# Attention weights transposed by VectorE blocks and GpSimd-queue transfers in place of TensorE, and the head norm's power moved to ScalarE and VectorE, in a hybrid decoder layer

## The chip, the cores and the metric

One core of a Trainium2 chip runs the whole program once. The metric is device microseconds of that core: the median of three runs of the kernel before is 1500.87 us (1500.5 to 1500.92). Everything is float32; the large matrix products are done as three float32r products of a high and a low part.

## The reference, cut to what matters

The program computes one decoder layer on 256 tokens of width 2048. The part that the diff touches is the two attentions of the mixer.

```python
# differential attention, 8 heads, per block of 128 queries
sc = einsum('bhmqd,bhmkd->bhmqk', qi, kh) * scale          # two maps m of width 64
p = softmax(where(causal, sc, -inf))
a = p[:, :, 0] - lam * p[:, :, 1]
o = einsum('bhqk,bhkv->bhqv', a, vh)                       # then rms_norm(o, da_subln_g)
# stick-breaking attention, 8 heads
z = einsum('bhqd,bhkd->bhqk', qi, kh) * scale
a = where(strict, exp(log_sigmoid(z) + tail), 0.0)
o = einsum('bhqk,bhkd->bhqd', a, vh)
```

Around them stand a projection of 2048 to 10240 columns, two branch projections with sigmoid gates, an output projection, a cross-attention, and a gated feed-forward part of width 5632 with a convolution over tokens.

## The kernel before, in words

The work is a stream of units. One unit multiplies the 256 tokens with 512 weight columns: 16 slices of 128 rows, two token tiles, three products each, so 96 matmuls of 512 columns. Weights come by SP's DMA queue in pieces of 1 MB; `split_w` makes the high part on ScalarE (L179) and the low part on VectorE (L180), in three buffers each; `multiply` issues the products (L185 to L187).

The attentions run as Python generators beside that stream. `product` calls `tick()` after every 12 matmuls, and a tick resumes at most two generators that are due; the number that a generator yields is the ticks until it is due again. That sets the order of the text. On every engine but SP the order of the program is then chosen when it is built, by Tile's scheduler, which goes by the text's order and by when it reckons each instruction to be ready (L723); on the chip each engine's order is fixed.

The units come in the order qa0, ka0, va0, qa1, ka1, va1, qb0, kb0, vb0, qb1, kb1, vb1, then eight gate units. Behind each qa and ka unit `proj_T` brings out the product, `rope` turns it with eight GpSimd instructions (L244 to L249), and two ticks later TensorE transposes it (L275). Behind va0 and va1 two chains of two heads each start, one tick apart; behind vb0 and vb1 one chain of two pairs of heads.

A head (`diff_head`) forms its scores (L312, four products, eight instructions on TensorE), masks them, takes the row maxima, the exponentials (L324) and the weights in place (L330, L332). Two ticks later `attn_T` transposes the three 128x128 blocks of weights on TensorE into PSUM (L294 to L296) and VectorE copies them out (L298). One tick on, the products with v follow (L341 to L343), the sum of squares (L160), the mean (L348), GpSimd's power of -1/2 (L351) and the scaling (L354); two ticks on, the result is transposed (L359). A pair of stick-breaking heads (`stick_pair`) does the same with other weights (L380 to L400), two calls of `attn_T`, and the products at L410 to L412.

In the feed-forward part the kernel already transposes another way: `turn` (L129) turns 32x32 blocks on VectorE, and `regroup` (L138) moves the blocks to their partitions with 16 DMAs from the GpSimd queue.

Tiles come from pools: `wk` has 7 buffers under the tag w2, `b4` has 34 of 4 KB a partition, `ps_sm` has 4 PSUM banks for scores, transposes and attention outputs.

Of the kernel before, what the change touches and what calls it, by code (L numbers as in the profile page):

```python
# [9 lines left out]
F32 = mybir.dt.float32  # L10
F32R = mybir.dt.float32r
AF = mybir.ActivationFunctionType
ALU = mybir.AluOpType
# [3 lines left out]
P = 128  # L17
S = 256
NT = S // P
# [26 lines left out]
def hybrid_layer(ctx: ExitStack, tc: tile.TileContext, x, xT, mem, memT, gmix, par, gfin,  # L46
                 w_in, w_pa, w_pb, w_out, w_xq, w_xkv, w_xo, w_up, w_dn, out):
    nc = tc.nc
# [58 lines left out]
    def chunk_tile(name, shape):  # L107
        return b4.tile(shape, F32, tag="b4", name=name)

    def sm_tile(name):  # L110
        return ps_sm.tile([P, U], F32, tag="sm", name=name)
# [175 lines left out]
            nc.scalar.activation(out=dst[:, t, :], in_=ps[t], func=AF.Copy, scale=r[:, t:t + 1])  # L287
        return dst

    def attn_T(a, name):  # L290


        pt = sm_tile(f"{name}_tp")
        nc.tensor.transpose(out=pt[:, 0:P], in_=a[0][:, 0:P], identity=ident)  # L294
        nc.tensor.transpose(out=pt[:, P:2 * P], in_=a[1][:, 0:P], identity=ident)
        nc.tensor.transpose(out=pt[:, 2 * P:3 * P], in_=a[1][:, P:2 * P], identity=ident)  # L296
        aT = wk.tile([P, 3 * P], F32, tag="w2", name=f"{name}_aT")
        nc.vector.tensor_copy(out=aT, in_=pt[:, 0:3 * P])  # L298
        return aT


    oaT = [None] * 4
# [1 line left out]
    def diff_head(h):  # L304
        qT, kT, v, hh = qa[h // 4], ka[h // 4], va[h // 4], h % 4

        at = (slice(0, P), slice(P, 3 * P))
        sc = [sm_tile(f"sa{m}") for m in range(2)]
        nm = st.tile([P, 2, NT], F32, tag="nm", name="nm")
        for m in range(2):  # L310
            for i in range(NT):
                nc.tensor.matmul(sc[m][:, at[i]], lhsT=qT[m * 64:(m + 1) * 64, hh, i * P:(i + 1) * P],  # L312
                                 rhs=kT[m * 64:(m + 1) * 64, hh, 0:(i + 1) * P], start=True, stop=True)
            dg = sc[m].rearrange("p (i k) -> p i k", i=2)[:, :, 0:P]
            nc.vector.tensor_tensor(out=dg, in0=dg, in1=mask_le.unsqueeze(1).broadcast_to([P, 2, P]),
                                    op=ALU.add)
            for i in range(NT):
                nc.vector.tensor_reduce(out=nm[:, m, i:i + 1], in_=sc[m][:, at[i]], op=ALU.max,
                                        axis=AX, negate=True)
        p = [wk.tile([P, 3 * P], F32, tag="w2", name=f"pa{m}") for m in range(2)]  # L320
        sm = st.tile([P, 2, NT], F32, tag="sm", name="sm")
        for m in range(2):
            for i in range(NT):
                nc.scalar.activation(out=p[m][:, at[i]], in_=sc[m][:, at[i]], func=AF.Exp,  # L324
                                     bias=nm[:, m, i:i + 1], scale=1.0, accum_out=sm[:, m, i:i + 1])
        nc.vector.reciprocal(out=sm, in_=sm)
        nc.vector.tensor_scalar(out=sm[:, 1], in0=sm[:, 1], scalar1=nlam, scalar2=None, op0=ALU.mult)
        aw = []
        for i in range(NT):
            nc.vector.tensor_scalar(out=p[0][:, at[i]], in0=p[0][:, at[i]], scalar1=sm[:, 0, i:i + 1],  # L330
                                    scalar2=None, op0=ALU.mult)
            nc.vector.scalar_tensor_tensor(out=p[0][:, at[i]], in0=p[1][:, at[i]],  # L332
                                           scalar=sm[:, 1, i:i + 1], in1=p[0][:, at[i]],
                                           op0=ALU.mult, op1=ALU.add)
            aw.append(p[0][:, at[i]])
        yield 2
        aT = attn_T(aw, "da")
        yield 1
        vc = slice(hh * P, (hh + 1) * P)
        po = sm_tile("oa").rearrange("p (t d) -> p t d", d=P)  # L340
        nc.tensor.matmul(po[:, 0], lhsT=aT[:, 0:P], rhs=v[:, 0, vc], start=True, stop=True)  # L341
        nc.tensor.matmul(po[:, 1], lhsT=aT[:, P:2 * P], rhs=v[:, 0, vc], start=True, stop=False)
        nc.tensor.matmul(po[:, 1], lhsT=aT[:, 2 * P:3 * P], rhs=v[:, 1, vc], start=False, stop=True)  # L343
        ss = st.tile([P, NT, 1], F32, tag="ss_o", name="ss_o")
        for t in range(NT):
            sumsq(ss[:, t], po[:, t])
        tot = st.tile([P, NT], F32, tag="st_o", name="st_o")
        nc.vector.tensor_scalar(out=tot, in0=ss[:, :, 0], scalar1=1.0 / P, scalar2=EPS,  # L348
                                op0=ALU.mult, op1=ALU.add)
        ro = st.tile([P, NT], F32, tag="ro", name="ro")  # L350
        nc.gpsimd.tensor_tensor(out=ro, in0=tot, in1=mhalf[:, :NT], op=ALU.pow)  # L351
        o = wk.tile([P, NT, P], F32, tag="w2", name="o")
        for t in range(NT):
            nc.vector.tensor_scalar(out=o[:, t], in0=po[:, t], scalar1=ro[:, t:t + 1], scalar2=None,  # L354
                                    op0=ALU.mult)
        yield 2
        pt = sm_tile("oaT")
        for t in range(NT):
            nc.tensor.transpose(out=pt[:, t * P:(t + 1) * P], in_=o[:, t], identity=ident)  # L359
        j = h % 2  # L360
        if oaT[h // 2] is None:
            oaT[h // 2] = act_tile(f"oaT{h // 2}")
        dst = oaT[h // 2]
        nc.scalar.activation(out=dst[:, 0, j], in_=pt[:, 0:S], func=AF.Copy, scale=gsub)
        nc.vector.scalar_tensor_tensor(out=dst[:, 1, j], in0=pt[:, 0:S], scalar=gsub,
                                       in1=dst[:, 0, j].bitcast(F32), op0=ALU.mult,
                                       op1=ALU.subtract)
# [2 lines left out]
    obT = [None] * 4  # L370

    def stick_pair(g):
        aw = [[], []]
        for i in range(NT):
            K = (i + 1) * P
            ps = sm_tile("sb")
            z = ps.rearrange("p (m k) -> p m k", m=2)
            for m in range(2):
                h = 2 * g + m
                nc.tensor.matmul(z[:, m, 0:K], lhsT=qb[h // 4][:, h % 4, i * P:(i + 1) * P],  # L380
                                 rhs=kb[h // 4][:, h % 4, 0:K], start=True, stop=True)
            dg = z[:, :, i * P:K]
            nc.vector.tensor_tensor(out=dg, in0=dg, in1=mask_lt.unsqueeze(1).broadcast_to([P, 2, P]),
                                    op=ALU.add)
            l = wk.tile([P, 2, S], F32, tag="w2", name="lb")
            nc.scalar.activation(out=l[:, :, 0:K], in_=z[:, :, 0:K], func=AF.Abs)
            nc.scalar.activation(out=l[:, :, 0:K], in_=l[:, :, 0:K], func=AF.Exp, scale=-1.0)
            nc.scalar.activation(out=l[:, :, 0:K], in_=l[:, :, 0:K], func=AF.Ln, bias=1.0)

            nc.vector.scalar_tensor_tensor(out=l[:, :, 0:K], in0=z[:, :, 0:K], scalar=0.0,  # L390
                                           in1=l[:, :, 0:K], op0=ALU.max, op1=ALU.add)
            c = wk.tile([P, 2, S], F32, tag="w2", name="cb")
            for m in range(2):
                nc.vector.tensor_tensor_scan(out=c[:, m, 0:K][:, ::-1], data0=ones[:, 0:K],
                                             data1=l[:, m, 0:K][:, ::-1], initial=0.0,
                                             op0=ALU.mult, op1=ALU.add)
            nc.vector.tensor_tensor(out=c[:, :, 0:K], in0=z[:, :, 0:K], in1=c[:, :, 0:K],
                                    op=ALU.subtract)
            a = wk.tile([P, 2, S], F32, tag="w2", name="ab")
            nc.scalar.activation(out=a[:, :, 0:K], in_=c[:, :, 0:K], func=AF.Exp)  # L400
            for m in range(2):
                aw[m].append(a[:, m, :])
        yield 3
        aT = [attn_T(aw[m], "sb") for m in range(2)]
        yield 1
        po = sm_tile("ob").rearrange("p (m s) -> p m s", m=2)
        for m in range(2):
            h = 2 * g + m
            v, vc = vb[h // 4], slice((h % 4) * P, (h % 4 + 1) * P)
            nc.tensor.matmul(po[:, m, 0:P], lhsT=v[:, 0, vc], rhs=aT[m][:, 0:P], start=True, stop=True)  # L410
            nc.tensor.matmul(po[:, m, P:S], lhsT=v[:, 0, vc], rhs=aT[m][:, P:2 * P], start=True, stop=False)
            nc.tensor.matmul(po[:, m, P:S], lhsT=v[:, 1, vc], rhs=aT[m][:, 2 * P:3 * P], start=False,  # L412
                             stop=True)
        obT[g] = act_tile(f"obT{g}")
        split(obT[g], po)
# [183 lines left out]
    for i in range(KF // 2):  # L599
        ps = product(x2T, w_up, i, KD, f"up{i}")  # L600
        blk = flip_tile(f"up{i}")
# [126 lines left out]
```

## Time and profile before

| | |
|---|---|
| median of 3 runs | 1500.87 us |
| the profiled execution's own time | 1501.38 us |
| its span, first to last instruction | 1499.6 us |
| TensorE busy | 1484.7 us (99%) |
| VectorE, ScalarE, GpSimd busy | 919.5, 781.6, 256.2 us |
| mean granted TensorE clock | 0.999 |

Busy time is the union of an engine's instructions. Matmuls are pipelined, so that an instruction's length on TensorE is longer than the time by which it puts off the next one; what a matmul costs the stream is read from how far apart the ends of neighbours stand.

### The profile page before, as it was taken

What the parts mean: (1) busy time and instruction counts of PE and PEld (TensorE: products, weight loads), DVE (VectorE), ACT (ScalarE), POOL (GpSimd) and SP (SyncE); (2) the same over time, 40 slices, a digit from 0 to 9 for tenths busy, and PEclk for the clock granted to TensorE, in tenths of its full rate; (3) what the DMA queues carried; (4) which work ended last, traced back from release to release, by engine and by line L of the source; (5) the groups of instructions that cost most, each with busy time, mean ns of one, the idle gap of its engine ahead of it and who ended that gap; (6) DMA issues with size and microseconds to landing.
All of it is one profiled execution on the core that took longest, in us unless ns stands there. A gap on an engine that the chain in (4) does not pass through costs nothing.

```text
span 1499.6 us, 17849 instructions
## 1 busy us (share of the span) xinstructions
PE 1484.7 (99%) x6728; PEld 1225.4 (82%) x6728; DVE 919.5 (61%) x1175; ACT 781.6 (52%) x1074; POOL 256.2 (17%) x424
## 2 busy tenths in 40 slices
PE   8999999999999999999999999999999999999997
PEld 6878788888888888888888888888888888888886
DVE  5566666565444555665676677767777776644562
ACT  6454455456444444664565555556655655444441
POOL 0202000000000010000003344334434433000010
PEclk9999999999999999999999999999999999999999
DMA  9544444545555556765445666666676666655561
GB/s 346 188 150 169 160 149 169 171 168 194 191 189 189 189 201 212 274 233 177 166 163 194 228 218 219 218 220 225 197 234 217 216 208 223 221 197 196 199 231 75
DMA packets 55270, 299.35 MB, mean 200 GB/s; under 512 B 10640, under 2 KB 10640, under 8 KB 22416
## 3 DMA queue, kind: packets, MB, share of 16 engines
q1 hardware_dynamic: 43488, 286.13, 54.8%
q0 software_dynamic: 11264, 11.56, 3.0%
q8 instruction: 52, 0.85, 0.2%
q10 hardware_dynamic: 432, 0.53, 0.1%
q14 instruction: 34, 0.28, 0.1%
HBM read 284.54 MB, written 2.10 MB: 191 GB/s over the span
## 4 chain that ended last, share of the span: by engine, by line
PE 98%; issue 1%; DMA 1%; DVE 0%; ACT 0%; SPq 0%; POOLq 0%; POOL 0%; DVEq 0%
PE up_mm L185 11%; PE up_mm L187 11%; PE up_mm L186 11%; PE dn_mm L186 5%; PE dn_mm L187 5%; PE dn_mm L185 5%; PE g_mm L185 4%; PE g_mm L187 4%; PE g_mm L186 4%; PE wo_mm L187 2%; PE wo_mm L186 2%; PE wo_mm L185 2%; PE va_mm L186 1%; PE qb_mm L186 1%; PE qb_mm L185 1%; PE kb_mm L187 1%
## 5 line engine op out<-in xcount | busy, mean ns | idle before, releaser
L180 DVE TENSOR_TENSOR up_lo<-up_raw,up_hi 128x1024 fp32r<-128x1024 f32 x176 | 214.5, 1223 | 130.7 <-ACT up_hi L179 130.7
L179 ACT CAST up_hi<-up_raw 128x1024 fp32r<-128x1024 f32 x176 | 184.9, 1050 | 192.2 <-PE up_mm L187 176.0
L187 PE MATMUL up_mm<-up_hi,x2T 128*128 128x512 f32 x704 | 273.9, 389 | 0.0
L186 PE MATMUL up_mm<-up_lo,x2T 128*128 128x512 f32 x704 | 273.9, 389 | 0.0
L138 POOL DMA_DIRECT2D uT<-up_blk x352 | 202.5, 583 | 287.8 <-DVE up_blk L129 169.1
L185 PE MATMUL up_mm<-up_hi,x2T 128*128 128x512 f32 x704 | 246.1, 389 | 0.0
L180 DVE TENSOR_TENSOR dn_lo<-dn_raw,dn_hi 128x1024 fp32r<-128x1024 f32 x88 | 109.8, 1253 | 94.9 <-ACT dn_hi L179 89.8
L187 PEld LDWEIGHTS up_mm<-up_hi,x2T 128*128 128x128 f32 x704 | 132.1, 188 | 27.5
L185 PEld LDWEIGHTS up_mm<-up_hi,x2T 128*128 128x128 f32 x704 | 132.2, 188 | 27.3
L186 PEld LDWEIGHTS up_mm<-up_lo,x2T 128*128 128x128 f32 x704 | 132.1, 188 | 27.4
L179 ACT CAST dn_hi<-dn_raw 128x1024 fp32r<-128x1024 f32 x88 | 91.8, 1054 | 115.2 <-PE dn_mm L187 99.9
L186 PE MATMUL dn_mm<-dn_lo,gT 128*128 128x512 f32 x352 | 136.9, 389 | 0.0
L187 PE MATMUL dn_mm<-dn_hi,gT 128*128 128x512 f32 x352 | 136.9, 389 | 0.0
L180 DVE TENSOR_TENSOR g_lo<-g_raw,g_hi 128x1024 fp32r<-128x1024 f32 x64 | 78.4, 1225 | 83.9 <-ACT g_hi L179 83.9
L185 PE MATMUL dn_mm<-dn_hi,gT 128*128 128x512 f32 x352 | 125.9, 389 | 0.0
L179 ACT CAST g_hi<-g_raw 128x1024 fp32r<-128x1024 f32 x64 | 67.2, 1051 | 73.5 <-PE g_mm L187 70.3
L186 PE MATMUL g_mm<-g_lo,hT 128*128 128x512 f32 x256 | 100.0, 391 | 0.0
L187 PE MATMUL g_mm<-g_hi,hT 128*128 128x512 f32 x256 | 99.8, 390 | 0.0
L185 PE MATMUL g_mm<-g_hi,hT 128*128 128x512 f32 x256 | 90.7, 391 | 0.0
L185 PEld LDWEIGHTS dn_mm<-dn_hi,gT 128*128 128x128 f32 x352 | 66.1, 188 | 13.8
L186 PEld LDWEIGHTS dn_mm<-dn_lo,gT 128*128 128x128 f32 x352 | 66.1, 188 | 13.8
L187 PEld LDWEIGHTS dn_mm<-dn_hi,gT 128*128 128x128 f32 x352 | 66.0, 188 | 13.6
(301 smaller groups left out, 2702.8 us busy)
## 6 DMA issues: line engine op xcount, KB each, us to landing
up_raw<-in_w_up SPq DMA_DIRECT2D x88, 1024.0 KB, 5.2
dn_raw<-in_w_dn SPq DMA_DIRECT2D x44, 1024.0 KB, 4.9
g_raw<-in_w_in SPq DMA_DIRECT2D x32, 1024.0 KB, 4.8
wo_raw<-in_w_out SPq DMA_DIRECT2D x16, 1024.0 KB, 4.9
uT<-up_blk POOLq DMA_DIRECT2D x352, 32.0 KB, 3.8
ka_raw<-in_w_in SPq DMA_DIRECT2D x8, 1024.0 KB, 6.3
va_raw<-in_w_in SPq DMA_DIRECT2D x8, 1024.0 KB, 4.8
qb_raw<-in_w_in SPq DMA_DIRECT2D x8, 1024.0 KB, 4.8
```

Source lines behind the costliest of these rows:

```text
L138: nc.gpsimd.dma_start(out=d[b * q:(b + 1) * q, :, a * q:(a + 1) * q], in_=s[a * q:(a + 1) * q, :, b * q:(b + 1) * q])
L179: nc.scalar.copy(out=hi, in_=src)
L180: nc.vector.tensor_tensor(out=lo, in0=src, in1=hi.bitcast(F32), op=ALU.subtract)
L185: nc.tensor.matmul(out, lhsT=a[0], rhs=b[0], start=start, stop=False)
L186: nc.tensor.matmul(out, lhsT=a[0], rhs=b[1], start=False, stop=False)
L187: nc.tensor.matmul(out, lhsT=a[1], rhs=b[0], start=False, stop=stop)
```

## The change

The weights of both attentions are no longer transposed on TensorE. VectorE turns their 32x32 blocks within SBUF into a tile `blk`, and `swap` moves each of the 16 combinations of partition group and column group with one DMA from the GpSimd queue into the tile `aT`, which the products with v read. Both tiles come from the pool `b4`; before, the transposed weights took a PSUM bank and a `wk` buffer. A head now yields 9 ticks between its weights and its products with v (before 2 and 1), a pair also 9 (before 3 and 1). In the head norm GpSimd's power becomes a logarithm and an exponential on ScalarE and four VectorE instructions (one Newton step).

```diff
-    def attn_T(a, name):
-        pt = sm_tile(f"{name}_tp")
-        nc.tensor.transpose(out=pt[:, 0:P], in_=a[0][:, 0:P], identity=ident)
-        nc.tensor.transpose(out=pt[:, P:2 * P], in_=a[1][:, 0:P], identity=ident)
-        nc.tensor.transpose(out=pt[:, 2 * P:3 * P], in_=a[1][:, P:2 * P], identity=ident)
-        aT = wk.tile([P, 3 * P], F32, tag="w2", name=f"{name}_aT")
-        nc.vector.tensor_copy(out=aT, in_=pt[:, 0:3 * P])
-        return aT
+    def swap(dst, blk):
+        q = P // 4
+        d, s = (v.rearrange("p (f c) -> p f c", c=P) for v in (dst, blk))
+        for a in range(4):
+            for b in range(4):
+                nc.gpsimd.dma_start(out=d[b * q:(b + 1) * q, :, a * q:(a + 1) * q],
+                                    in_=s[a * q:(a + 1) * q, :, b * q:(b + 1) * q])
...
     def diff_head(h):
...
-        yield 2
-        aT = attn_T(aw, "da")
-        yield 1
+        blk = chunk_tile("da_blk", [P, 3 * P])
+        nc.vector.transpose(out=blk, in_=p[0])
+        aT = chunk_tile("da_aT", [P, 3 * P])
+        swap(aT, blk)
+        yield 9
...
-        nc.gpsimd.tensor_tensor(out=ro, in0=tot, in1=mhalf[:, :NT], op=ALU.pow)
+        nc.scalar.activation(out=ro, in_=tot, func=AF.Ln)
+        nc.scalar.activation(out=ro, in_=ro, func=AF.Exp, scale=-0.5)
+        nc.vector.tensor_tensor(out=tot, in0=tot, in1=ro, op=ALU.mult)
+        nc.vector.tensor_tensor(out=tot, in0=tot, in1=ro, op=ALU.mult)
+        nc.vector.tensor_scalar(out=tot, in0=tot, scalar1=-0.5, scalar2=1.5, op0=ALU.mult, op1=ALU.add)
+        nc.vector.tensor_tensor(out=ro, in0=ro, in1=tot, op=ALU.mult)
...
     def stick_pair(g):
-        aw = [[], []]
+        blk = chunk_tile("sb_blk", [P, 2, 3 * P])
...
             for m in range(2):
-                aw[m].append(a[:, m, :])
-        yield 3
-        aT = [attn_T(aw[m], "sb") for m in range(2)]
-        yield 1
+                nc.vector.transpose(out=blk[:, m, i * P:i * P + K], in_=a[:, m, 0:K])
+        aTs = chunk_tile("sb_aT", [P, 2, 3 * P])
+        swap(aTs.rearrange("p m k -> p (m k)"), blk.rearrange("p m k -> p (m k)"))
+        aT = [aTs[:, m] for m in range(2)]
+        yield 9
```

## Rows read from the trace of the kernel before

**Rows 1.** The page, busy time of TensorE: us (share of the span), instructions.
```profile
PE 1484.7 (99%) x6728; PEld 1225.4 (82%) x6728; DVE 919.5 (61%) x1175; ACT 781.6 (52%) x1074; POOL 256.2 (17%) x424
```
**Rows 2.** The page, the chain that ended last, by engine.
```profile
PE 98%; issue 1%; DMA 1%; DVE 0%; ACT 0%; SPq 0%; POOLq 0%; POOL 0%; DVEq 0%
```
**Rows 3.** Stretch 400 to 500 us: busy us (instructions) of PE, PEld, DVE, ACT, POOL; clock; DMA.
```profile
400.00:500.00 100.00, 100.00 (x443) 82.81 (x442) 44.88 (x37) 49.93 (x52) 0.00 (x0) 1.00 0.57 198
```
**Rows 4.** Timeline of TensorE around one head's transposes: start, length (us), instruction.
```profile
120.47 0.38 PE L341 MATMUL oa<-va,da_aT 128*128 128x128 f32 x2
...
120.91 0.39 PE L343 MATMUL oa<-va,da_aT 128*128 128x128 f32 x2
121.14 0.27 PE L294 MATMUL da_tp<-ident,pa 128*128 128x128 f32 x1
121.25 0.27 PE L295 MATMUL da_tp<-ident,pa 128*128 128x128 f32 x1
121.36 0.27 PE L296 MATMUL da_tp<-ident,pa 128*128 128x128 f32 x1
121.38 0.49 PE L186 MATMUL ka_mm<-ka_lo,hT 128*128 128x512 f32 x1
```
**Rows 5.** The tile da_tp: length in ns min/median/max, first and last start.
```profile
L294 PE MATMUL da_tp<-ident,pa x8: 270/272/273, 87.0 to 201.2; 128*128 128x128 f32 x8
```
**Rows 6.** Timeline of TensorE, scores of the fourth head.
```profile
109.91 0.39 PE L186 MATMUL ka_mm<-ka_lo,hT 128*128 128x512 f32 x1
110.14 0.38 PE L359 MATMUL oaT<-ident,o 128*128 128x128 f32 x2
110.45 0.93 PE L312 MATMUL sa<-kaT,qaT 64*128 64x128 f32 x8
111.31 0.50 PE L187 MATMUL ka_mm<-ka_hi,hT 128*128 128x512 f32 x1
```
**Rows 7.** Timeline of TensorE, first scores of the fifth head, inside unit va1.
```profile
144.71 0.61 PE L185 MATMUL va_mm<-va_hi,hT 128*128 128x512 f32 x2
145.26 0.48 PE L312 MATMUL sa<-kaT,qaT 64*128 64x128 f32 x2
145.67 0.50 PE L186 MATMUL va_mm<-va_lo,hT 128*128 128x512 f32 x1
```
**Rows 8.** The tile uT: the feed-forward part's transfers, length in ns; time to landing.
```profile
L138 POOL DMA_DIRECT2D uT<-up_blk x352: 582/582/775, 797.1 to 1265.3; - x176
...
DMA to landing us min/median/max: 1.8/3.8/6.5
```
**Rows 9.** Timeline of VectorE: end of the weights of the third and fourth head, copy between.
```profile
109.66 0.74 DVE L332 SCALAR_TENSOR_TENSOR pa<-pa,sm,pa 128x128 f32<-128x128 f32 x2
...
115.50 0.55 DVE L298 COPY da_aT<-da_tp 128x384 f32<-128x384 f32 x1
...
116.79 0.96 DVE L332 SCALAR_TENSOR_TENSOR pa<-pa,sm,pa 128x128 f32<-128x128 f32 x2
```
**Rows 10.** The tile up_blk: VectorE's block transposes in the feed-forward part.
```profile
L129 DVE STREAM_TRANSPOSE up_blk<-up_mm x44: 695/716/718, 795.0 to 1254.4; 128x512 f32<-128x512 f32 x44
```
**Rows 11.** Head norm: GpSimd's power, ScalarE's squares, VectorE's mean (length in ns).
```profile
L351 POOL TENSOR_TENSOR ro<-st_o,mhalf x8: 689/690/711, 95.8 to 211.4; 128x2 f32<-128x2 f32 x8
...
L160 ACT ACTIVATE junk<-oa x16: 268/270/278, 94.9 to 209.6; 128x128 f32<-128x128 f32 x16
...
L348 DVE TENSOR_SCALAR st_o<-ss_o x8: 159/166/170, 95.5 to 211.2; 128x2 f32<-128x2 f32 x8
```
**Rows 12.** Waits from 60 to 360 us: who for whom, us in total, times, longest.
```profile
ACT va_hi L179 <- PE va_mm L187: 16.4, 9, 2.6
```
**Rows 13.** Timeline of GpSimd: first and last of unit ka1's eight rope instructions.
```profile
132.97 0.42 POOL L244 TENSOR_TENSOR rope_a<-kaT_z,pc 128x128 f32<-128x128 f32 x1 [0.92 <-ACT kaT_z L266]
...
136.68 1.50 POOL L249 TENSOR_TENSOR kaT_z<-rope_a,rope_b 128x128 f32<-128x128 f32 x1
```
**Rows 14.** Timeline of TensorE: the last transposes of unit ka1.
```profile
139.92 0.60 PE L275 MATMUL kaT_tp<-ident,kaT_z 128*128 128x128 f32 x4
```

More of the change, by code (lines that the diff above doesn't have):

```diff
@@ L327, in diff_head @@
         nc.vector.tensor_scalar(out=sm[:, 1], in0=sm[:, 1], scalar1=nlam, scalar2=None, op0=ALU.mult)
-        aw = []
         for i in range(NT):
@@ L334, in diff_head @@
                                            op0=ALU.mult, op1=ALU.add)
-            aw.append(p[0][:, at[i]])
-        yield 2
-        aT = attn_T(aw, "da")
-        yield 1
+        blk = chunk_tile("da_blk", [P, 3 * P])
[3 more added lines that the diff above has]
+        yield 9
         vc = slice(hh * P, (hh + 1) * P)
```

## The prediction

> **What bounds the kernel now.** I read four views in this order. The busy times [rows 1] put TensorE at 99% of the span and the next engine at 61%. The chain of waits [rows 2] says the same from the other end: 98% of what ended last is TensorE's own work, and the 1% of issue and 1% of DMA are the load before the first product. So an instruction taken off TensorE is worth what it holds up the stream, and an instruction added elsewhere costs nothing until TensorE waits for it. A stretch with weight products alone gives the price of one of them: 100 us by 443 is 0.226 us [rows 3]. The timeline of TensorE then shows what the attention puts between them, and which of it goes.
>
> **What leaves TensorE.** Each of the 8 heads loses three transposes, each of the 4 pairs six: 48. Three in a row [rows 4]: the product before them ends at 120.91 + 0.39 = 121.30, the weight product behind them at 121.38 + 0.49 = 121.87; without them 121.30 + 0.226 = 121.53. So three cost 0.34 us, one 0.115, and 48 cost 5.5 us. That they hold up the stream, and are not hidden in it, is what these ends show.
>
> A row of another kind gives another price: one transpose lasts 270 ns from its start to its end [rows 5]. The Trainium skill (TensorE: Matmul & The Clock Gate, Part 4: PE-mode transpose) says that in one kernel's context a 128x128 transpose took about 275 ns. The duration here agrees with that; by it the sum would lose 48 x 0.275 = 13.2 us and come to 1487.7. The starts in rows 4 stand 0.11 us apart, so the measurement decides for 0.115.
>
> **What the change adds, and what hides it.**
>
> VectorE: a block transpose for 384 columns replaces a copy of 0.55 us [rows 9]. The nearest row is 0.716 us for 512 columns out of PSUM [rows 10]; by columns that is 0.54 us, so nothing changes for a head. A pair has four narrower transposes in place of two copies, perhaps 0.5 us more. Bounds per head: -0.2 and +0.2 us, off the path.
>
> Head norm: out of GpSimd's 0.69 us come two ScalarE instructions of at most 0.27 and four of VectorE of about 0.17 [rows 11], 1.2 us a head, 0.5 more than before, while ScalarE's queue waits once for VectorE's mean. Behind it stand the casts of weights. They have slack: ScalarE itself waits for TensorE to give a buffer back, up to 2.6 us at a time [rows 12]. Free as long as that wait is there; without it 0.5 us for each of 8 heads, 4 us.
>
> GpSimd and DMA: 16 transfers for each of 12 groups, 192. At 0.582 us [rows 8] a group takes 9.3 us of an engine that is busy for 17% [rows 1]. The last lands 3.8 us after its issue (1.8 to 6.5). For a first head that is, from its scores: 7.3 us to its weights (110.45 to 117.75, rows 6 and 9), 0.54, 9.3, 3.8, together 21 us, inside the 9 ticks of 12 products, 24.4 us. The second head of a chain's pair starts a tick (2.7 us) later, but its transfers queue behind the first's: 7.3 + 0.54 + 2 x 9.3 + 3.8 - 2.7 = 27.5 us, 3.1 too late by the text. A pair of stick-breaking heads has the same 9.3 us and a longer way to its weights.
>
> That lateness costs nothing, because TensorE does not keep the text's order. By the text the fourth head's transposes come 2 ticks, 5.4 us, after its scores; they stand 10.7 us after them, 3.4 us behind the end of its weights [rows 4, 6, 9]. The third head's products with v stand at 120.47, 4.4 us behind the end of the copy at 116.05 [rows 4, 9]. So the order is built around when things are ready, with some 4 us to spare, and weight products fill in. Added waits on landing: below nothing is excluded, as a wait frees no time; above, one group could be late by 6.5 - 4.4 = 2.1 us. Behind that wait on TensorE stand the weight products of the running unit, and behind those the rest of the kernel, so a wait there would be paid in full. I take 0.
>
> Buffers: a group takes two of the 34 in b4, four for two heads at once. Live beside them are 8 of the input, at most 9 of q, k and v, 8 of attention outputs and, behind vb1, the gates as they come; that is 29 before the gates and less than 34 until the last pair is through, so no load of weights waits. A PSUM bank and a wk buffer come free earlier than now. Price 0; with the pool full a head would start later, and nobody waits for it until the branch projections.
>
> **Where the scores fall.** The change moves the heads in the text: one takes 12 ticks in place of 6. The eight score instructions of a head cost more or less by how they fall. In one go [rows 6]: from 109.91 + 0.39 = 110.30 to 111.31 + 0.50 = 111.81, less 0.226 and less two transposes of 0.115, is 1.05 us. Put singly between weight products [rows 7]: 146.17 - 145.32 - 0.226 = 0.62 us for a quarter of them, the wider quarters not less, so 2.5 us or more a head. Heads that run ahead of their place in the text fall into pieces (the fifth does, inside va1), heads at their place or behind it come in one go (the fourth). If all that ran ahead came in one go, this would give some 4 us; if the third, fourth, seventh and eighth head, now in one go, fell apart, it would take 4 x 1.45 = 5.8 us. I take 0, since the nearest row to each head is its own of before; both ends are in the range.
>
> **Sum.** Against the profiled execution: 1501.38 - 5.5 = 1495.9. The median of the runs is 1500.87, 0.5 lower than that execution, so 1495.4 for the median, 0.37% faster. The smallest change that a measurement tells from none is 0.2%, 3.0 us.
>
> **Rival 1, slower: rope behind the transfers.** GpSimd's queue is in order too. By the text the second group of heads comes 6 ticks (16.3 us) later than now, so the third head's weights end at 110.40 + 16.3 = 126.7 and its 16 transfers run from 127.2 to 136.5. Unit ka1's rope is ready at 133.0 [rows 13], and the fourth head's transfers, ready at 117.75 + 16.3 + 0.5 = 134.6, stand ahead of it in the text. If they go first, rope starts at 145.8 instead of 133.0 and lasts 5.2 us, to 151.0. The transposes that read it stand at 139.92 now [rows 14]; if TensorE's order keeps them there, it waits 11 us once, and the time is 1495.4 + 11 = 1506.4. It decides once that wait is over 8.5 us. Against it: the same order by readiness as above. For it: the order is fixed when the program is built, and no row shows a GpSimd queue with both kinds of work. First group and second half are not hit: no head's transfers run at qa1's rope, and qb and kb have none.
>
> **Rival 2, no change: scores in pieces.** With six of the transposes and copies gone from each group's way, TensorE has room ahead of the third, fourth, seventh and eighth head, and fills it with their scores one by one. Price as above: 1495.4 + 5.8 = 1501.2; with half of it 1498.3. For it: the fifth head does this wherever a unit leaves a gap. Against: before, the third and fourth could have done so and did not.
>
> **Rival 3, no change: late transfers.** If TensorE waits for landing at three of the 12 groups by 2.1 us, it gives back 6.3 us: 1501.7. A mechanism for it is a GpSimd that can't issue while VectorE holds it off; the longest of 352 issues is 0.775 us against 0.582 [rows 8], with VectorE doing the same splits, so 16 of the longest make a group 3.1 us later. The Trainium skill (SBUF — State Buffer, SBUF: two separate sides) has a rule for it: while VectorE runs a two-port operation, GpSimd is kept from writing descriptors. By that rule this change is a bad trade; the trace of the feed-forward part speaks against it here, with a median at the minimum of 582 ns.
>
> **Rival 4, no change: nothing was held up.** If TensorE's instructions fill only time in which it waits for weights, taking 48 away gives nothing: 1500.9. Rows 4 speak against it: the product behind them starts 0.34 us later.
>
> **How the numbers follow.** The forecast, with scores a little better or worse, 0.60; rival 1 0.08; rival 2 0.20 (a quarter of it, with half the price, still under 1497.9); rival 3 0.06; rival 4 0.06. Faster by over 0.2% is below 1497.87: 0.60 + 0.05 = 0.65. Slower by over 0.2% is above 1503.87: 0.08. The rest, 0.27, is within. The range goes from 1491.6 (all scores that ran ahead in one go) to 1501.0, which takes in most of rivals 2 and 4 and leaves out rival 1 and the worst of rival 3. The forecast's own range is 1491.6 to 1497.8.
>
> **What would show it.** Right: TensorE's line has 48 transposes fewer (6680 of 6728) and its weight products still end 0.226 us apart everywhere from 60 to 360 us; products with v stand some us behind the last landing; GpSimd is busy for about 256 + 112 - 5 = 363 us. Wrong by rival 1: a gap in front of ka1's transposes, ended by rope. By rival 2: scores in rows of two between weight products for the third, fourth, seventh and eighth head. By rival 3: gaps in front of the products with v, ended by a DMA. By a slow norm: ScalarE's casts late and TensorE waiting for the low part of weights.

## The result, and the profile after

The changed kernel takes 1544.02 us (1543.18 to 1545.31) where the kernel before takes 1500.87: a ratio of 1.0288, 95% interval 1.0277 to 1.03. The forecast was 1495.4. The profiled execution took 1543.18 us, 41.8 more than that of before.

The page of the changed kernel: busy times, TensorE and its granted clock in 40 slices of 38.5 us, and the chain that ended last by engine.

```profile
PE 1489.8 (97%) x6680; PEld 1229.1 (80%) x6680; DVE 926.5 (60%) x1215; ACT 789.2 (51%) x1094; POOL 355.1 (23%) x608
...
PE   8999897879799999999999999999999999999997
...
PEclk9999998989899999999999999999999999999999
...
PE 95%; DVE 2%; ACT 2%; issue 1%; DMA 0%; SPq 0%; POOLq 0%; POOL 0%; DVEq 0%; ACTq 0%
```

Against [rows 1, 2]: 48 instructions left TensorE, as they should, and yet it is busy for 97% and not 99%, with holes from the fifth slice to the eleventh, which lie in the mixer. For what it waits there, from 60 to 460 us (in the kernel before this list is empty): who for whom, us in total, times, longest.

```profile
PE kbT_tp L275 <- ACT kbT_z L266: 14.3, 2, 9.5
PE g_mm L185 <- ACT gate L287: 8.8, 1, 8.8
PE vb_mm L185 <- ACT qbT_z L266: 6.3, 1, 6.3
PE oaT L364 <- DVE o L359: 6.2, 2, 3.2
PE kb_mm L185 <- ACT va L287: 1.2, 1, 1.2
```

None of the five is a transfer. Four are evacuations: ScalarE's copies that bring a finished unit out of PSUM, into z (L266) or into v and the gates (L287); the fifth is a head's result `o`, for which its transposes wait. The timeline of ScalarE around the copy of ka1 and three of the four (start, length, instruction, idle time before it):

```profile
141.47 0.48 ACT L322 ACTIVATE pa<-sa,nm 128x256 f32<-128x256 f32 x1
141.83 0.21 ACT L322 ACTIVATION_READ_ACCUMULATOR pa<-sa,nm 128x1 f32 x1
141.92 1.28 ACT L266 ACTIVATE kaT_z<-ka_mm,r 128x512 f32<-128x512 f32 x2
...
297.72 0.63 ACT L405 ACTIVATE ab<-cb 128x512 f32<-128x512 f32 x1 [3.40 <-DVE cb L402]
298.26 1.25 ACT L266 ACTIVATE qbT_z<-qb_mm,r0b 128x512 f32<-128x512 f32 x2
...
335.29 0.63 ACT L405 ACTIVATE ab<-cb 128x512 f32<-128x512 f32 x1 [2.79 <-DVE cb L402]
335.83 1.25 ACT L266 ACTIVATE kbT_z<-kb_mm,r 128x512 f32<-128x512 f32 x2
...
404.53 1.28 ACT L392 ACT_TABLE_LOAD   x1
...
418.40 0.63 ACT L405 ACTIVATE ab<-cb 128x512 f32<-128x512 f32 x1 [1.49 <-DVE cb L402]
418.93 1.25 ACT L287 ACTIVATE gate<-g_mm,r 128x512 f32<-128x512 f32 x2
```

And the timeline of TensorE: the last product of unit qb1, the first pair of stick-breaking heads (scores sb, products ob, next scores), the end of the first gap above, and ka1's transposes.

```profile
174.54 1.04 PE L275 MATMUL kaT_tp<-ident,kaT_z 128*128 128x128 f32 x8
...
268.06 0.39 PE L187 MATMUL qb_mm<-qb_hi,hT 128*128 128x512 f32 x1
...
283.23 1.48 PE L385 MATMUL sb<-kbT,qbT 128*128 128x128 f32 x8
...
298.98 0.80 PE L185 MATMUL vb_mm<-vb_hi,hT 128*128 128x512 f32 x1 [6.27 <-ACT qbT_z L266]
299.57 0.63 PE L186 MATMUL vb_mm<-vb_lo,hT 128*128 128x512 f32 x1
300.00 0.63 PE L187 MATMUL vb_mm<-vb_hi,hT 128*128 128x512 f32 x1
...
322.25 0.38 PE L416 MATMUL ob<-sb_aT,vb 128*128 128x128 f32 x2
...
324.46 0.61 PE L385 MATMUL sb<-kbT,qbT 128*128 128x128 f32 x4
```

Unit qb1 is through at 268.45, but its copy out of PSUM stands in ScalarE's order behind the last exponential of the stick pair, at 298.26. In the meantime unit kb1 takes the other two of the four banks of `ps_mm`, and TensorE has nowhere to put vb1. The other gaps are alike: they lie in five holes between units, and at the end of each the next unit starts 0.7 to 1.5 us after the start of such a copy (kb0 at 181.85 after va1's from 181.1, qb1 at 244.3 after kb0's from 242.8, and so on). The last hole has something more. ScalarE loads its function tables five times between 404 and 417 us, 1.28 us each: a gate's sigmoid (L484) now runs ahead of the last pair's exponentials and logarithms. ScalarE is busy for 12.6 of these 13 us, and the gate's copy stands behind them. The fast versions further down (y16, y20, four) have the same five loads in that pair and no gap, so that the loads alone don't make one; how much of the 8.8 us is theirs no run separates. By the ends of neighbouring matmuls (those more than 0.5 us apart, less the 0.226 us of a product), nine gaps hold 39.9 us. After a gap the next products stand 0.43 us apart, as at 299.57 and 300.00, in place of 0.226 [rows 3]. The whole stretch, and two short ones behind the gap at 243 us for their granted clock (columns as in [rows 3]; the clock is the third number from the end):

```profile
60.00:460.00 400.00, 363.13 (x1644) 295.76 (x1643) 218.36 (x357) 191.20 (x311) 114.39 (x208) 0.95 0.47 160
244.30:246.20 1.90, 1.90 (x7) 1.51 (x6) 1.32 (x3) 0.91 (x2) 1.90 (x5) 0.50 0.12 24
246.70:248.70 2.00, 2.00 (x10) 1.66 (x9) 0.00 (x0) 0.00 (x0) 2.00 (x4) 1.00 0.10 22
```

At 0.50 the array runs at 1.2 GHz, at 1.00 at 2.4. The Trainium skill (TensorE: Matmul & The Clock Gate, Part 1: The HAM clock gate) has an idle array fall to the lower level and gives 426.7 ns from one 512-column product to the next there; the trace agrees. It hits 37 products, 37 x 0.2 = 7.4 us. So 39.9 + 7.4 - 5.5 for the transposes is 41.8, which is the difference of the two profiled executions.

What was added costs what was expected. The tiles of the transfers, of the block transposes and of the norm (length in ns; time to landing):

```profile
L296 POOL DMA_DIRECT2D da_aT<-da_blk x128: 545/545/750, 83.5 to 261.0; - x128
L296 POOL DMA_DIRECT2D sb_aT<-sb_blk x64: 565/567/581, 302.7 to 428.5; - x64
...
DMA to landing us min/median/max: 1.6/2.9/6.1
...
L334 DVE STREAM_TRANSPOSE da_blk<-pa x8: 570/572/578, 82.6 to 244.5; 128x384 f32<-128x384 f32 x8
...
L407 DVE STREAM_TRANSPOSE sb_blk<-ab x16: 269/356/446, 292.0 to 419.4; 128x128 f32<-128x128 f32 x8, 128x256 f32<-128x256 f32 x8
...
L351 ACT ACTIVATE ro<-st_o x8: 203/203/204, 110.2 to 284.5; 128x2 f32<-128x2 f32 x8
```

### The profile page after: what moved, and what is told of

It is laid out like the page before. It is cut to its first block, busy times and chain, and to the rows that moved or that the text cites. A ratio compares the mean times of both kernels' runs of the same rounds, so it can differ in the third digit from the quotient of the medians.

```text
span 1541.1 us, 18128 instructions
## 1 busy us (share of the span) xinstructions
PE 1489.8 (97%) x6680; PEld 1229.1 (80%) x6680; DVE 926.5 (60%) x1215; ACT 789.2 (51%) x1094; POOL 355.1 (23%) x608
## 4 chain that ended last, share of the span: by engine, by line
PE 95%; DVE 2%; ACT 2%; issue 1%; DMA 0%; SPq 0%; POOLq 0%; POOL 0%; DVEq 0%; ACTq 0%
PE up_mm L186 10%; PE up_mm L185 10%; PE up_mm L187 10%; PE dn_mm L187 5%; PE dn_mm L185 5%; PE dn_mm L186 5%; PE g_mm L185 4%; PE g_mm L186 4%; PE g_mm L187 4%; PE wo_mm L185 2%; PE wo_mm L187 2%; PE wo_mm L186 2%; PE vb_mm L185 1%; PE va_mm L186 1%; PE vb_mm L186 1%; PE vb_mm L187 1%
## 5 line engine op out<-in xcount | busy, mean ns | idle before, releaser
L185 PEld LDWEIGHTS up_mm<-up_hi,x2T 128*128 128x128 f32 x704 | 132.1, 188 | 27.5
L185 PE MATMUL g_mm<-g_hi,hT 128*128 128x512 f32 x256 | 93.5, 398 | 8.9 <-ACT gate L287 8.8
L187 PE MATMUL g_mm<-g_hi,hT 128*128 128x512 f32 x256 | 101.1, 396 | 0.0
L296 POOL DMA_DIRECT2D da_aT<-da_blk x128 | 69.3, 549 | 91.1 <-DVE da_blk L334 56.5
L187 PEld LDWEIGHTS dn_mm<-dn_hi,gT 128*128 128x128 f32 x352 | 66.1, 188 | 13.7
```

What stands on the lines that cost most here:

```text
L185: nc.tensor.matmul(out, lhsT=a[0], rhs=b[0], start=start, stop=False)
L187: nc.tensor.matmul(out, lhsT=a[1], rhs=b[0], start=False, stop=stop)
L296: nc.gpsimd.dma_start(out=d[b * q:(b + 1) * q, :, a * q:(a + 1) * q], in_=s[a * q:(a + 1) * q, :, b * q:(b + 1) * q])
```

## The experiments

The theories named in the expectations. **Claim theory**, formed after the first four runs: the order of each engine is fixed when the program is built, and where tiles share a pool, they are handed out in the order of the text. A head or pair that waits for its transfers holds up what comes behind it in the text: its own o and oaT, the next head's scores and weights, and with them a unit's evacuation. **Buffer theory**: the pools are too small. **Queue theory**: GpSimd's one stream of transfers and rotations makes the heads late. **Latency**, **Rhythm**, **Port**, **Pool**, **Bank** and **Norm theory** are told in the expectations.

| kernel | us | ratio, 95% interval |
|---|---|---|
| norm_only | 1499.5 | 0.9993, 0.9983 to 1.0002 |
| swap_only | 1538.6 | 1.0252, 1.0235 to 1.0269 |
| yields | 1496.98 | 0.9977, 0.9968 to 0.9986 |
| wk9 | 1544.41 | 1.0291, 1.0276 to 1.0307 |
| y12 | 1503.92 | 1.0024, 1.0014 to 1.0033 |
| y16 | 1493.05 | 0.9952, 0.9937 to 0.9967 |
| y20 | 1494.85 | 0.9962, 0.9947 to 0.9977 |
| yields16 | 1499.11 | 0.9989, 0.998 to 0.9999 |
| four | 1495.09 | 0.9963, 0.995 to 0.9976 |
| early9 | 1526.29 | 1.0177, 1.016 to 1.0194 |
| z_tag | 1536.88 | 1.0243, 1.0228 to 1.0258 |
| pre4z | 1536.2 | 1.0241, 1.0224 to 1.0258 |
| own | 1544.35 | 1.0286, 1.0269 to 1.0303 |
| da_swap | 1531.77 | 1.021, 1.0195 to 1.0225 |
| y16_pow | 1496.04 | 0.9969, 0.9958 to 0.9981 |

### Which part costs

norm_only: the new norm alone, on the kernel before.

```diff
-        nc.gpsimd.tensor_tensor(out=ro, in0=tot, in1=mhalf[:, :NT], op=ALU.pow)
+        nc.scalar.activation(out=ro, in_=tot, func=AF.Ln)
+        nc.scalar.activation(out=ro, in_=ro, func=AF.Exp, scale=-0.5)
...
```

> The kernel before with the head norm alone changed (power on ScalarE and VectorE). Buffer theory (ScalarE brings projections out of PSUM only when a w2 work buffer is free; heads and pairs now hold those buffers at the wrong time): no change, 1498 to 1504 us. Queue theory (16 transfers a group on GpSimd, and what stands behind them, are late): no change, the same. Norm theory (ScalarE's queue, waiting for VectorE twice a head, holds back casts and evacuations): most of the loss is here, over 1520.

swap_only: the reverse edit, on the changed kernel.

> The changed kernel with the old head norm (GpSimd's power), which now queues on GpSimd behind transfers. Buffer theory: as the changed kernel or some us slower, 1535 to 1560 us, since the scaled head holds its buffer until the power is done. Queue theory: slower than the changed kernel, over 1550. Norm theory: under 1525.

yields: on the kernel before, transposes stay on TensorE, in the rhythm of the change.

```diff
-        yield 2
         aT = attn_T(aw, "da")
-        yield 1
+        yield 9
...
```

> The kernel before with transposes still on TensorE and the old norm, but with the new rhythm: no ticks between weights and transposes, 9 ticks between transposes and products with v. Buffer theory: the copied weights hold a w2 buffer for those 9 ticks more, so that it is short of buffers too, 1510 to 1550 us. Queue theory: no transfers, so 1498 to 1504. Norm theory: 1498 to 1504.

wk9: the changed kernel with more work buffers.

```diff
-    b4 = ctx.enter_context(tc.tile_pool(name="b4", bufs=34))
-    wk = ctx.enter_context(tc.tile_pool(name="wk", bufs=7))
+    b4 = ctx.enter_context(tc.tile_pool(name="b4", bufs=33))
+    wk = ctx.enter_context(tc.tile_pool(name="wk", bufs=9))
```

> The changed kernel with 9 w2 work buffers in place of 7, and 33 b4 buffers in place of 34 to pay for them. Buffer theory: evacuations come at once, the gaps of 3 to 10 us before kbT's transposes, unit vb and a gate unit go, 1494 to 1505 us. Queue theory: the transfers are as late as before, 1530 to 1545. Norm theory: as queue theory.

The norm alone costs nothing, the rhythm alone gains 3.6 us (1496.98 against the 1500.57 of the kernel before beside it), and two more work buffers change nothing: the waits of TensorE in wk9 are those of the changed kernel, kbT_z with 14.1 us, the gate with 8.8, qbT_z with 6.3. The loss belongs to the transfers in this rhythm. Within it the new norm has some 5.4 us (1544.02 against 1538.6).

### The distance between transfers and products

y16, y12 and y20: one number in two places of the changed kernel.

```diff
-        yield 9
+        yield 16
```

> Edit on the changed kernel: 16 ticks for 9 between a head's or pair's transfers and its products with v (yield 16). Claim theory: the tiles that a head or pair asks for after its transfers (o, oaT, obT) come later in the text than one more evacuation, so fewer evacuations stand behind a late transfer: at least a third of the 43 us comes back, 1505 to 1530 us. Latency theory: the products are later still and so is what they feed; 1544 us or slower. Queue theory: transfers and rotations keep their order on GpSimd, 1540 to 1548 us.

> Edit on the changed kernel: 12 ticks for 9 between transfers and products. Claim theory: 12 ticks are 32.6 us, which is about what the second head of two needs (27.5 us by the prediction's own working, and more in the planner's order, where products stand 30 to 40 us behind the weights), so some evacuations are on time and some not: between the two, 1500 to 1535 us. Rhythm theory (the result depends on which tiles happen to meet and not on the length): anything, also over 1544 us.

> Edit on the changed kernel: 20 ticks for 9 between transfers and products. Claim theory: with 16 ticks no evacuation was late any more, so 20 give nothing further, and a little back where the later products put off the next heads: 1490 to 1500 us. Rhythm theory: 16 was a lucky place, 20 may lose again, over 1505 us.

yields16: the edit of yields with 16.

> Edit on the kernel before: its TensorE transposes stay, with 16 ticks between them and the products with v. It says how much of the gain with 16 ticks (1493.05 us) comes from the transposes that left TensorE and how much from the rhythm. By the prediction's price of 0.115 us for each of 48 transposes: 5.5 us more than with 16 ticks and transfers, 1498.5 (1496 to 1501). If the gain was rhythm alone: 1491 to 1495 us.

Sixteen ticks give back 51 us and beat the kernel before by 0.48%. Latency theory falls: in y16 the products with v stand further behind their transfers than with 9, and nothing waits. The stretch from 60 to 460 us of y16, to be held against the same stretch of the changed kernel above, and whose list of TensorE's waits is empty again:

```profile
60.00:460.00 400.00, 400.00 (x1861) 328.03 (x1861) 239.66 (x375) 215.38 (x335) 113.37 (x208) 1.00 0.54 184
```

GpSimd is as busy in both. What differs is when units leave PSUM. In the changed kernel ka1's copy is the one at 141.92 in ScalarE's timeline above, behind the fourth head's exponentials (L322); its last product had started at 124.8. ScalarE's timeline in y16:

```profile
123.86 1.31 ACT L266 ACTIVATE kaT_z<-ka_mm,r 128x512 f32<-128x512 f32 x2 [1.04 <-PE ka_mm L187]
```

There the copy waits for TensorE alone. Nine ticks are 24.4 us, twelve 32.5, sixteen 43.4. In the changed kernel the pair that starts at 283.23 has its products at 322.25 and hands on to the next at 324.46, 41 us; but a gap of 6.3 us lies within them, and the distance that is needed can't be read off from this: with twelve ticks the first pair takes 48 us from scores to products and has no gap behind it, and only two gaps of 4 us stay, both ahead of oaT.

What the missing transposes are worth is not y16 against yields16, 6.1 us, since yields16 has the old norm. With the old norm in both, y16_pow (below) against yields16, the same rhythm without and with transposes on TensorE, it is 1499.11 - 1496.04 = 3.1 us.

### The number of transfers

four: a quarter of the transfers, the same bytes, at 9 ticks. It leaves out the move between partitions, so that the weights are not fully transposed and the layer's result is not formed; it shows time alone.

```diff
         for a in range(4):
-            for b in range(4):
-                nc.gpsimd.dma_start(out=d[b * q:(b + 1) * q, :, a * q:(a + 1) * q],
-                                    in_=s[a * q:(a + 1) * q, :, b * q:(b + 1) * q])
+            nc.gpsimd.dma_start(out=d[:, :, a * q:(a + 1) * q], in_=s[:, :, a * q:(a + 1) * q])
```

> Edit on the changed kernel: 4 transfers for 16 in each group, each over all 128 partitions, so that a column group stays on its partitions: left out is the move between partitions. Bytes, rhythm (9 ticks), buffers and norm stay. Claim theory (a head's tiles behind its transfers come ahead of the next unit's evacuation in the text; as long as the transfers are reckoned and run longer than the 9 ticks, the evacuation waits for them): with 4 issues of some 0.6 us the group is through in about 2.4 us and its landing, inside the 9 ticks, so the evacuations are on time: no gap of TensorE over 2 us, 1493 to 1502 us. Rhythm theory (9 ticks put the tiles in a bad order in the text whatever the transfers take): over 1530 us. Port theory (VectorE's block transposes or the transfers' bytes hold others up): the bytes are the same, over 1530 us.

1495.09, no gap. One issue is longer, but four are 3.0 us where sixteen are 8.7. Rhythm and Port theory fall: ticks, bytes and block transposes are those of the changed kernel. The tile in four:

```profile
L295 POOL DMA_DIRECT2D da_aT<-da_blk x32: 757/757/947, 83.6 to 215.2; - x32
```

So the loss takes both, sixteen transfers a group and products nine ticks behind them, and either end can be moved. On the chip the transfers need not be longer than the ticks: those of the first two heads have landed 16 and 23 us after the heads' scores. What the order reckoned them at when it was built, no run shows.

### What the late units stand behind

early9: units take their result tiles at their start.

```diff
+    def claimed(name):
+        dst = chunk_tile(name, [P, NT, U])
+        nc.vector.memset(dst[:, 0, 0:1], 0.0)
+        return dst
...
+        dst = claimed(f"va{i}")
-        va[i] = proj_n(unit(4 + i, f"va{i}"), r0, f"va{i}")
+        va[i] = proj_n(unit(4 + i, f"va{i}"), r0, f"va{i}", dst)
...
```

> Edit on the changed kernel: each projection unit takes its result tiles (z, v, gate) at the start of the unit instead of at its end, each marked by a one-column VectorE memset; the work pool gets 9 buffers for 7, the pool of chunks 33 for 34. Transfers, rhythm and norm stay. Claim theory (the buffers of a pool are given out in the order of the text; a unit's evacuation, asked for at the unit's end, stands behind tiles of heads that wait for their transfers, so the PSUM banks stay full and TensorE has no unit to work on): the evacuations follow their unit at once, the eight gaps of TensorE (some 41 us together) mostly go, 1494 to 1510 us. Queue theory (GpSimd's one stream of transfers and rotations is late, and with it the heads): the stream is the same, over 1530 us. Latency theory (the 20 to 40 us that a head or pair waits for its transfers leave TensorE without work in whatever order buffers are given out): over 1530 us.

z_tag: z no longer shares w2 with the heads.

```diff
-            z = wk.tile([P, U], F32, tag="w2", name=f"{name}_z")
+            z = wk.tile([P, U], F32, tag="z", name=f"{name}_z", bufs=2)
...
```

> Edit on the changed kernel: the projection result z that is to be transposed gets a pool tag of its own with two buffers, in place of a share of the work tag w2 (chunks 33 for 34). v and gate results stay where they were. Claim theory: the gaps of TensorE that end on the evacuation into z (at 243, 299 and 337 us in the changed kernel, 5.3 + 7.1 + 10.0 us = 22 us, with the smaller ones next to them up to 28 us) go, those that end on v and gate (9.6 us at 420) stay: 1514 to 1528 us. Queue theory and Latency theory: no change, 1538 to 1549 us.

pre4z: z_tag, and the four oaT are taken ahead of all units.

```diff
-    oaT = [None] * 4
+    oaT = [claimed_out(f"oaT{i}") for i in range(4)]
...
```

> Edit on the changed kernel: z in a tag of its own with two buffers (as in the run z_tag), and the four tiles oaT of the differential heads are taken ahead of all units, each marked by a one-column VectorE memset; b4 33 for 34. In the built order of ScalarE this moves the evacuation of va1 from behind 60 casts of weights (63 in z_tag) to behind 51, where the kernel before has it; those of vb0 and later stay late. Claim theory (va1's tile in b4 stood behind oaT of the third and fourth head): va1 leaves its PSUM banks at 152 to 156 us (181.1 in the changed kernel, 186.0 in z_tag), no gap of TensorE over 1 us between 60 and 240 us, and the gaps of the pairs stay: 1518 to 1536 us. Bank theory (the heads' PSUM banks, not the tiles, hold up the stream): 1535 to 1546 us, gaps ahead of oaT at 180 to 240 us stay.

own: the transfers' tiles leave b4.

```diff
-        blk = chunk_tile("da_blk", [P, 3 * P])
+        blk = swap_tile("da_blk")[:, 0]
...
```

> Edit on the changed kernel: the tiles of the transfers (blk and aT) come from a pool of their own with 5 less 1 = 4 buffers, and b4 gets 31 for 34. Rhythm, transfers and norm stay. Pool theory (v and the gates are late because the buffer they get in b4 was that of a transfer that has still to land): they no longer meet there, the gaps that end on v and gate (2.0 us at 182, 9.6 us at 420) go, 1528 to 1536 us. Claim theory with text order (what a head asks for behind its products, o and oaT, and the next head's tiles still come ahead of the evacuation): the order of the evacuations stays, 1538 to 1548 us.

The sizes were missed in three of four: early9 brings back 18 us where 34 to 50 were expected, z_tag 7 where 16 to 30 were, pre4z ends 0.2 us outside its range. What early9 was to do, it did in part only: the marks that take the tiles stand late themselves. Unit qb1 starts at 224.6, its mark stands here in VectorE's timeline, and its copy follows at 285.59:

```profile
285.48 0.07 DVE L263 MEMSET qbT_z<- 128x1 f32 x2
```

The copies of ka1 and va1 moved as Claim theory has it; the time that they were to bring back did not follow. In z_tag the copy of ka1 moves from 141.92 to 126.12 (in wk9, with more buffers of the shared tag, it stays at 142.2), that of va1, whose tile is in b4, stays late at 186.0. With oaT out of its way as well, in pre4z (timeline of ScalarE, then the stretches from 60 to 240 and from 240 to 460 us, then TensorE):

```profile
152.21 1.37 ACT L287 ACTIVATE va<-va_mm,r 128x512 f32<-128x512 f32 x2 [0.98 <-PE va_mm L187]
```

```profile
60.00:240.00 180.00, 180.00 (x829) 145.20 (x828) 107.89 (x184) 86.06 (x153) 60.64 (x112) 1.00 0.53 181
240.00:460.00 220.00, 184.12 (x847) 151.61 (x846) 114.29 (x176) 109.46 (x160) 53.07 (x96) 0.92 0.44 148
```

```profile
184.23 0.39 PE L347 MATMUL oa<-va,da_aT 128*128 128x128 f32 x2
...
192.51 1.57 PE L315 MATMUL sa<-kaT,qaT 64*128 64x128 f32 x12
...
325.22 0.77 PE L419 MATMUL ob<-sb_aT,vb 128*128 128x128 f32 x2 [24.21 <-DMA sb_aT<-sb_blk]
```

The first half is whole: TensorE is busy for all of the 180 us. The second half pays instead. The next heads' scores still stand behind the products of the heads before (192.51 behind 184.23; in y16 they start at 153.53, ahead of those products at 188.70), so the pairs come late, and a gap of 24 us is new: TensorE waits for the landing of the first pair's transfers, and it has no unit to run, since vb1 is done and z has only two buffers, so that kb1's result leaves PSUM behind qb1's transposes, which start at 327.9 behind the pair's products (ScalarE's timeline):

```profile
329.01 0.69 ACT L266 ACTIVATE kbT_z<-kb_mm,r 128x512 f32<-128x512 f32 x1 [0.27 <-PE qbT_tp L275]
```

That the scores wait for a bank of `ps_sm` is read from the order alone, and neither a third buffer for z nor more banks were tried. So Claim theory is shown for the first half, by moving two copies; for the second half it is argued.

Pool theory falls with own as the account of the loss: the time is unchanged, 1544.35. It has a part in one gap: the 8.8 us ahead of a gate unit shrink to 1.3, while the 1.2 ahead of kb0, behind the copy of va1, stay. In their place TensorE waits for the last pair's transfers (own, waits of TensorE from 395 to 460 us):

```profile
PE ob L420 <- DMA sb_aT<-sb_blk: 5.6, 1, 5.6
PE g_mm L189 <- ACT gate L291: 1.3, 1, 1.3
```

Queue theory falls too: in pre4z ka1's rotation is done by 130.6 us, where the changed kernel ends it at 166.6, and still the time is 1536.

### Half of the transfers, and the norm in the better rhythm

da_swap: the pairs go back to `attn_T` and their old rhythm.

```diff
-        swap(aTs.rearrange("p m k -> p (m k)"), blk.rearrange("p m k -> p (m k)"))
-        aT = [aTs[:, m] for m in range(2)]
-        yield 9
+        yield 3
+        aT = [attn_T(aw[m], "sb") for m in range(2)]
+        yield 1
...
```

> Edit on the changed kernel: the four stick pairs go back to TensorE transposes with their old rhythm (3 ticks, then 1); the eight differential heads keep VectorE blocks and GpSimd transfers. Four pairs have half of the transposes (24 of 48). Claim theory: the late evacuations from 299 us on stood behind pairs, so the gaps at 299, 337 and 420 us (7.1 + 10.0 + 9.6 = 27 us) mostly go, those of the heads (180 to 244 us, 14 us) stay: 1508 to 1522 us. Queue theory (the rotation of ka1 behind transfers of heads is what costs): the rotation stays behind the heads' transfers, 1530 to 1545 us. Latency theory: the loss follows the transfers, half of them: about 1522 us.

1531.77, in the range that Queue theory gave and outside the other two. The gaps of the heads are there (ahead of oaT 6.2 us, kbT_z 4.7, va 1.2), and from 295 to 313 us TensorE waits another 12.7 us for the first pair's exponentials, although the pairs have no transfers: it has no unit to run in the meantime, since the copies of qb1 and kb1 out of PSUM come only at 313.2 and 314.3. So the heads alone cost 31 us, and their lateness reaches the pairs.

y16_pow: y16 with GpSimd's power.

> Edit on the kernel with 16 ticks: the head norm's power goes back to GpSimd, one instruction for six. In the rhythm of 9 ticks the new norm made 5.4 us (1544.02 against 1538.6), alone on the kernel before nothing (0.9993). Norm theory (it costs ScalarE and VectorE time that a kernel with transfers feels): 2 to 5 us faster than with 16 ticks, 1488 to 1491. Claim theory (the norm only lengthens a head's way to the tiles that evacuations wait for, and with 16 ticks none waits): the same within 2 us, 1491 to 1495 us.

1496.04, 3.0 slower than y16, which neither theory gave: with the power a gap of 0.9 us stands ahead of oaT at 300 us, and where the rest goes wasn't traced. So the new norm's price has no sign of its own. It costs 5.4 us with 9 ticks, nothing on the kernel before, and gains 3 with 16.

## Why the prediction was wrong

**What leaves TensorE** was about right: 0.115 us by the ends of neighbours, 5.5 us in all, and with it the sum of the gaps above closes. The one comparison that changes only how the weights are transposed, yields16 against y16_pow, gives 3.1, with a gap of 0.9 in y16_pow against it. The 275 ns that the Trainium skill (TensorE: Matmul & The Clock Gate, Part 4: PE-mode transpose) gives for one transpose, taken as a price, 13.2 us in all, is too much here.

**What the change adds** was right in size. Block transposes: 0.572 us against an estimate of 0.54. Issues: 0.545 to 0.567 us for an assumed 0.582 [rows 8]. GpSimd is busy for 355 us against 363. From scores to landing the first two heads take 16.1 and 22.7 us where the prediction reckoned 21 and 27.5. The norm in itself: ScalarE's two instructions 0.2 us each, VectorE's four 0.16; put at nothing (4 us without slack on ScalarE), it cost 5.4 us in this rhythm. Where the scores fall, put at 0 too: the new rhythm alone gains 3.6 us with 9 ticks and 1.7 with 16 (yields, yields16), a size for which no trace was read.

**Where it failed: "That lateness costs nothing, because TensorE does not keep the text's order".** The prediction took one distance of 4.4 us between a copy and its products as the built order's habit. With transfers it is another: the first head's last transfer is issued by 93.5 us and lands at most 6.1 later, at 99.6, and its products stand at 107.6; the second head's is out by 103.8 and its products stand at 126.2, at least 16 us behind landing (GpSimd's last transfers, TensorE's first products of each head):

```profile
102.14 1.62 POOL L296 DMA_DIRECT2D da_aT<-da_blk  x3 [0.22 <-issue]
```

```profile
107.63 0.38 PE L340 MATMUL oa<-va,da_aT 128*128 128x128 f32 x2
...
126.25 0.39 PE L340 MATMUL oa<-va,da_aT 128*128 128x128 f32 x2
```

The order stands as if the transfers took longer than they do, and the pace of heads and pairs follows the order, 41 us a pair (gaps included) against the 24.4 that the text gives them. What was put at nothing came to 39.9 us of gaps and 7.4 at the lower clock.

**The second failing step is in the term for buffers: "nobody waits for it until the branch projections".** A late head holds its successors in the text, and the units' copies out of PSUM are among them. The prediction counted buffers, and count was not what failed as far as it was tried: wk9 adds two to w2, own takes the transfers out of b4, and neither moves the time. More room in b4 itself was not tried. What it did not price is who stands behind whom in a pool's order. So TensorE did not wait for a landing in any gap of the changed kernel; it ran out of PSUM two units later.

**Rival 1** saw half of it. Rope of ka1 does get behind the transfers. GpSimd's timeline:

```profile
142.76 0.48 POOL L244 TENSOR_TENSOR rope_a<-kaT_z,pc 128x128 f32<-128x128 f32 x1 [33.98 <-ACT kaT_z L266]
143.21 0.36 POOL L245 TENSOR_TENSOR rope_b<-kaT_z,pc 128x64 f32<-128x64 f32 x1
143.51 8.13 POOL L296 DMA_DIRECT2D da_aT<-da_blk  x15
...
158.22 4.30 POOL L296 DMA_DIRECT2D da_aT<-da_blk  x8 [0.48 <-DMA da_aT<-da_blk]
162.53 1.07 POOL L247 TENSOR_TENSOR rope_b<-kaT_z,pc 128x64 f32<-128x64 f32 x1
...
165.26 1.32 POOL L249 TENSOR_TENSOR kaT_z<-rope_a,rope_b 128x128 f32<-128x128 f32 x1
```

It starts 10 us later than in [rows 13], because z came late, and ends 28 us later, at 166.6; the transposes that read it move from 139.92 [rows 14] to 174.54. But no gap stands there: the order had moved them too. Its 11 us at that place are wrong, its side was right.

**Rival 3** did not come: TensorE waits for no transfer, and no issue is longer than 0.750 us. The lock that the Trainium skill (SBUF — State Buffer, SBUF: two separate sides) describes is not seen in these lengths. **Rival 2**, scores in pieces, has no share that shows; **rival 4** falls with y16_pow against yields16, 3.1 us apart in runs whose ranges don't meet.

## What to carry to other kernels

When a step gets a longer latency, don't only ask whether its own readers wait; ask what stands behind it in the text and shares a pool, a bank or a queue with it, and look in the trace for results that leave PSUM late. Then move the readers further off in the text (9 to 16 ticks: 51 us) or shorten the latency (16 to 4 transfers: 49 us, in a kernel that leaves out part of the move); two more work buffers did nothing. How far off is enough was found by trying, not by a rule. An engine that is full at 99% has no spare units to run when two of them can't leave PSUM, and the gaps also cost products behind them, which run at half clock.

## What was not expected

Sixteen ticks make the transfers a gain, 1493.05 us, the fastest version of the study, with every wait of TensorE in the mixer gone. A DMA over all 128 partitions takes GpSimd 0.757 us to issue where one over 32 takes 0.545, so that four wide ones cost a third of sixteen narrow ones for the same bytes, though not for the same move. And the price of an edit depends on the rhythm around it: the same six norm instructions cost 5.4 us, nothing, or gain 3.
